# A third raw weight buffer from the second chunk on, low parts of weights in program order, and operands loaded whole

## The chip, the cores and the metric

The kernel runs on one core of a Trainium2 chip. The metric is the device time of one execution in microseconds (us). Three runs of the kernel before took 1780.84, 1779.01 and 1780.94 us; their median is 1780.84.

The engines are named as in the profile: PE is TensorE (matrix products), PEld its weight loads, DVE is VectorE, ACT is ScalarE, POOL is GpSimd, SP is SyncE. SP does no arithmetic here; it issues most of the transfers (DMAs), and its instructions, like those of each engine, run strictly one behind the other. A DMA that has to wait holds up what is behind it in its queue. SPq in the profile's rows is this queue.

## The reference

One layer of a streaming encoder is applied to a prompt of 1024 frames and to a sample of 32 frames that share the weights; the model dimension is 1024 and all numbers are 32 bit floats. Cut to its core:

```python
h = rms_norm(x, g_mix)
z = h @ w_in                       # q, k, v, conv h/B/C, gates a and b
a = attn_core(q, k, v) @ w_attn_out
bo = (cb * conv) @ w_conv_out      # short causal convolution over cc * ch
x = x + (sigmoid(ga) * a + sigmoid(gb) * bo) @ w_mix_out
hc = rms_norm(x, g_cross)          # cross-attention to 256 memory tokens,
cq = hc @ w_cq                     # 4 heads of 64
p = softmax(cq . mem_k * 0.125)
x = x + (p . mem_v) @ w_co
hm = rms_norm(x, g_mlp)
x = x + square(relu(hm @ w_up)) @ w_down   # 1024 -> 4096 -> 1024
```

A final norm follows, and the new keys, values and convolution rows are outputs too.

## The kernel before, in words

**Columns and chunks.** The 1056 frames (prompt and sample together) are the columns of the moving operand. They are worked on in three chunks of 384, 384 and 288 columns; `c` in the code is the chunk. The model dimension is on the 128 partitions, in eight tiles (`f` from 0 to 7).

**High and low parts.** To keep 32 bit precision each operand is split into a high part, which TensorE takes at its fast 32 bit rate, and the low rest. A product is three matmuls: weight high by operand high, weight high by operand low, weight low by operand high (lines 193 to 195 for whole chunks of the trunk, 864 to 866 in the first half of the MLP). `split` makes the parts: ScalarE copies the raw tile into the high part (`wh` for a weight, line 129), VectorE subtracts that from the raw one for the low part (`wl`, line 130).

**Weights.** A weight comes as a tile of 128x1024, 512 KB. `fetch_w` issues its load into a raw buffer (line 155), `issue_w` splits it; two weights are prepared ahead of the one in use (`LOOK`). Raw tiles `wr` rotate over two buffers; while the dictionary `third` is filled, each third fetch goes into a tile of another pool instead (tag `ws`, named wr with two numbers in the order listings). That pool, `W["pool"]`, is shared with work on sums of weights, which GpSimd does and stores to DRAM (`usum_d`, `gsum_d`, `wsum_d`), so a tile of it is free only when such a store has read it. For the odd weights of the trunk the low part is stored to DRAM once (`wl_d`, line 172) and loaded again by later chunks (line 166), with the high part cast at line 167.

**Phases.** First the input projection and the windowed attention (up to about 640 us), then pairs of gate products (to about 800). Then the trunk, chunk by chunk: eight products with w_conv_out, eight with w_mix, from 809 us on; beside the trunk of chunk 1 goes the cross-attention of chunk 0, beside the trunk of chunk 2 that of chunk 1. From about 960 us on, products of a first part of w_up fill in as well; from about 1072 us on only they do, beside the cross-attention of chunk 2. The second part of w_up begins at about 1196 us, w_down at 1436.

**Cross-attention.** `do_cq` makes the queries: ScalarE and VectorE split them (lines 1113 and 1114). For a unit, `scores` issues score matmuls `sc` into one PSUM bank, VectorE takes the negative maximum `nmx` (1143), ScalarE the exponentials `S` (1145, with a load of its function table where another function came before), VectorE the reciprocal `rec` (1146) and the multiplications (1148). `turn` transposes them on TensorE (`pt`, 1157) and splits them, and `values` makes the products `o`. Then come the products with w_co (1203).

**The first part of w_up.** It works on half of the columns, in two quarters of 264: `xa[0]` and `xa[1]`. The operands come from `normed(c, f)` (line 1279), which also stores the normed chunk to DRAM (`xn_d`, line 1282). The second quarter, `xa[1]`, is columns 264 to 527 and so has 120 columns of chunk 0 and 144 of chunk 1. Its raw values are gathered in the tile of its low part (in a `Z` tile): 120 columns from xn_d at `open_first` (line 1229), 144 straight from the tile of `normed(1, f)` (line 1284). `second_split(f)` then splits them in place (lines 1296 and 1297).

**What sets the order.** Python code calls the operations in a program order, which is a list of items (`plan`) with small calls placed at numbered fillers (`then(i, ...)`). A scheduler behind it then orders each engine's instructions by its own estimate of times, and may move an instruction ahead of others on its engine. `pin` forbids that for one instruction: it has to stand behind the instruction of its engine that the program issued just before it.

Of the kernel before, what the change touches and what calls it, by code (L numbers as in the profile page):

```python
# [10 lines left out]
F32 = mybir.dt.float32  # L11
# [11 lines left out]
CH = [(0, 384), (384, 384), (768, 288)]  # L23
NF = 8
HT = 528
QT = 264
# [14 lines left out]
def hybrid_step(ctx: ExitStack, tc: tile.TileContext, io):  # L41
    nc = tc.nc
    act, dve, pool_e, pe, sp = nc.scalar, nc.vector, nc.gpsimd, nc.tensor, nc.sync
# [38 lines left out]
    xn_d = dram.tile([P, NF, NT], F32, name="xn_d")  # L82
# [14 lines left out]
    def pin(ins):  # L97
        return tc.keep_in_program_order(ins)
# [19 lines left out]
    def item(fn, *keys):  # L118
        plan.append((fn, keys))
        worder.extend(keys)  # L120
# [4 lines left out]
    ready = []  # L125
    wpos = [0]

    def split(hi, lo, src):
        act.copy(hi, src)  # L129
        dve.tensor_sub(lo, src, hi.bitcast(F32))  # L130

    def weight(key):
        name, *at = key
# [11 lines left out]
    third = {}  # L145
# [12 lines left out]
    def issue_w():  # L158
        if not fetched:
            fetch_w()  # L160
        raw = fetched.pop(0)
        key = worder[wpos[0]]
        hi = wp.tile([P, 1024], F32R, tag="wh", name=nm("wh"))
        lo = wp.tile([P, 1024], F32R, tag="wl", name=nm("wl"))
        if kept.get(key) is not None:
            sp.dma_start(lo.bitcast(F32), kept[key])
            act.copy(hi, raw)
        else:
            split(hi, lo, raw)
            if key in kept:  # L170
                kept[key] = dram.tile([P, 1024], F32, name=nm("wl_d"))
                sp.dma_start(kept[key], lo.bitcast(F32))
        ready.append((worder[wpos[0]], (hi, lo)))
        wpos[0] += 1
# [101 lines left out]
    W = {}  # L276
# [514 lines left out]
    def pump(n):  # L791
        for into, at, t, get in coming:
            hi, lo = into[at] = (get(), get())
            pin(act.copy(hi, t))
            pin(dve.tensor_sub(lo, t, hi.bitcast(F32)))
        coming.clear()
        for into, at, src, cols, get in wanted[:n]:
            t = cols() if callable(cols) else tmp(cols)
            sp.dma_start(t, src)
            coming.append((into, at, t, get))  # L800
        del wanted[:n]
# [216 lines left out]
    def after_gates():  # L1018
        nonlocal m_cm, mpool, cr_cm, cr
        assert not pieces and "new" not in W  # L1020
        closed(x_cm)
        xacc_tile()
        third.update(n=0, pool=W["pool"])
        m_cm, mpool = opened("mpool", bufs=18, reuse_waits="tile")
        cr_cm, cr = opened("cross", bufs=1, reuse_waits="tile", side="right")

# [194 lines left out]
    def open_first():  # L1221

        closed(m_cm)
        S["l"] = ctx.enter_context(tc.tile_pool(name="first", bufs=4, reuse_waits="tile"))
        S["z"] = ctx.enter_context(tc.tile_pool(name="second", bufs=8, reuse_waits="tile"))
        for f in range(NF):
            z = zslot()
            xa[1][f] = (quarter(z, 0), quarter(z, 1))
            sp.dma_start(xa[1][f][1].bitcast(F32)[:, : CH[0][1] - QT], xn_d[:, f, QT : CH[0][1]])
        for name in ("w_cq", "w_co"):  # L1230
            del kept[name, 1]

# [44 lines left out]
    def normed(c, f):  # L1277
        t = tmp(CH[c][1])
        pin(dve.scalar_tensor_tensor(t, x1[c][f], col(G_MLP + f), R[c], op0=ALU.mult, op1=ALU.mult))
        o, n = CH[c]  # L1280
        if c < 2 or f > 3:
            sp.dma_start(xn_d[:, f, o : o + n], t)
        if c == 1:
            sp.dma_start(xa[1][f][1].bitcast(F32)[:, CH[0][1] - QT :], t[:, : HT - CH[1][0]])
        if c == 2:
            top[f] = t
        if c == 0:
            hi, lo = (yslot(0)[:, :QT] for _ in range(2))
            xa[0][f] = (hi, lo)
            act.copy(hi, t[:, :QT])  # L1290
            pin(dve.tensor_sub(lo, t[:, :QT], hi.bitcast(F32)))

    def split_here(hi, lo):

        raw = lo.bitcast(F32)
        pin(act.copy(hi, raw))
        pin(dve.tensor_sub(lo, raw, hi.bitcast(F32)))

    def second_split(f):
        split_here(*xa[1][f])  # L1300
# [329 lines left out]
    def beside(steps, fillers, late=()):  # L1630
        for i, filler in enumerate(fillers):
            item(*filler)
            for x in [x for at, x in late if at == i]:
                item(lambda x=x: x())
            if steps:
                kind, what = steps.pop(0)
                for x in what:
                    if kind == "items":
                        item(*x)
                    else:  # L1640
                        item(lambda x=x: x())
        return steps
# [10 lines left out]
    trunks[0].insert(NF, trunks[1].pop(0))  # L1653
    left = beside([], trunks[0], [(i, lambda: pump(2)) for i in range(NF)])
    item(lambda: pump(0))
    left = beside(cross_steps(0), trunks[1])

    normeds = lambda c, at: [(at + f, lambda f=f: normed(c, f)) for f in range(NF)]
# [12 lines left out]
    def then(i, *what):  # L1671
        at.setdefault(i, []).extend(what)
# [14 lines left out]
    assert opened_at == 18  # L1687
    then(18, call(open_first))
    for f in range(NF):
        then(19 + f // 4, call(normed, 1, f))  # L1690
        then(22, call(second_split, f))
    then(19, call(chunk_col, 2))
    then(20, call(chunk_row, 2))
# [291 lines left out]
```

## Time and profile before

| | us |
|---|---|
| median of three runs | 1780.84 |
| profiled execution | 1778.09 |
| its span, first to last instruction | 1776.3 |
| PE busy | 1734.2 (98%) |
| VectorE busy | 1184.4 (67%) |
| ScalarE busy | 852.8 (48%) |
| GpSimd busy | 576.8 (32%) |

The profiled execution is one of the program's own; its span leaves out 1.8 us before the first and after the last instruction. Matmuls are pipelined: one of 264 columns is listed with some 0.28 us, but the next starts 0.12 us after it. The granted clock is the share of its full speed that TensorE was given; its mean over the execution is 0.99. In the rows of the timeline the first number is the start in us from the start of the span, the second the duration; at the end, in brackets, how long the engine had stood idle, and behind the arrow whom it had waited for.

### The profile page before, as it was taken

Reading aid. Unit: us, or ns where it says so; the run is one execution under the profiler, and the core shown is the slowest. Engines: PE = TensorE matmul, PEld = TensorE weight load, DVE = VectorE, ACT = ScalarE, POOL = GpSimd, SP = SyncE. Lnnn points to the kernel's source line nnn. Section 1 sums busy time; section 2 is a strip of 40 time slices with the busy share of each in tenths; the row PEclk is TensorE's granted clock in tenths of the full one; section 3 lists DMA queues with packets and bytes.
Section 4 is the critical chain, followed back from the end, with each engine's and each line's share of the span. In section 5 each row is a group of like instructions: output and inputs, shape, how many; then the busy total and the mean of one; then the engine's idle time right before and its main releaser. Section 6 shows DMA issues by size and latency. Waiting matters only on the chain.

```text
span 1776.3 us, 32569 instructions
## 1 busy us (share of the span) xinstructions
PE 1734.2 (98%) x12250; PEld 1716.3 (97%) x12250; DVE 1184.4 (67%) x2270; ACT 852.8 (48%) x1660; POOL 576.8 (32%) x651
## 2 busy tenths in 40 slices
PE   8999999999999999979999999999999999999998
PEld 8999999999999999979999989999999999999998
DVE  7776867868666647536667677786666686556575
ACT  8643534435335324324556665774444463333443
POOL 0025366543453444531225130004555510000121
PEclk9999999999999999989999998999999999999999
DMA  5333334333446888747765667575666686554554
GB/s 183 109 117 128 111 128 155 120 139 136 148 155 223 298 274 288 264 166 272 261 213 196 236 224 233 183 257 196 223 221 224 213 310 212 186 184 167 193 173 157
DMA packets 182221, 349.75 MB, mean 197 GB/s; under 512 B 19744, under 2 KB 102976, under 8 KB 181936
## 3 DMA queue, kind: packets, MB, share of 16 engines
q1 hardware_dynamic: 167008, 295.07, 49.1%
q0 software_dynamic: 15056, 52.60, 8.4%
q8 instruction: 96, 1.57, 0.4%
q14 instruction: 61, 0.50, 0.1%
HBM read 252.82 MB, written 94.19 MB: 195 GB/s over the span
## 4 chain that ended last, share of the span: by engine, by line
PE 77%; DMA 11%; POOL 6%; DVE 2%; issue 2%; ACT 2%; SPq 0%; DVEq 0%; POOLq 0%; ACTq 0%
PE acc L193 10%; PE acc L195 10%; PE acc L194 10%; PE acc L1772 6%; PE acc L1770 6%; PE acc L1771 6%; PE acc L864 5%; PE acc L866 5%; PE acc L865 5%; DMA wsum_d<-ws 3%; DMA wsum_d<-xacc 3%; POOL ws L719 2%; POOL xacc L719 2%; PE pc L864 2%; PE pc L865 2%
## 5 line engine op out<-in xcount | busy, mean ns | idle before, releaser
L129 ACT CAST wh<-wr 128x1024 fp32r<-128x1024 f32 x226 | 237.2, 1050 | 424.5 <-PE acc L1771 126.2
L130 DVE TENSOR_TENSOR wl<-wr,wh 128x1024 fp32r<-128x1024 f32 x226 | 292.5, 1294 | 140.6 <-ACT wh L129 138.6
L193 PE MATMUL acc<-X,wh 128*128 128x384 f32 (+1 forms) x864 | 281.8, 326 | 6.6 <-ACT wh L129 6.6
L194 PE MATMUL acc<-X,wh 128*128 128x384 f32 (+1 forms) x864 | 279.1, 323 | 0.0
L195 PE MATMUL acc<-X,wl 128*128 128x384 f32 (+1 forms) x864 | 278.5, 322 | 0.3 <-DVE wl L130 0.3
L269 POOL TENSOR_TENSOR xacc<-xacc,ct 128x384 f32<-128x384 f32 (+1 forms) x56 | 73.4, 1314 | 401.8 <-ACT ct L267 400.3
L193 PEld LDWEIGHTS acc<-X,wh 128*128 128x128 f32 x864 | 163.0, 189 | 7.2 <-ACT wh L129 6.6
L194 PEld LDWEIGHTS acc<-X,wh 128*128 128x128 f32 x864 | 163.1, 189 | 0.7
L195 PEld LDWEIGHTS acc<-X,wl 128*128 128x128 f32 x864 | 162.8, 188 | 0.9 <-DVE wl L130 0.8
L195 PE MATMUL acc<-Y,wl 128*128 128x384 f32 (+1 forms) x432 | 139.1, 323 | 1.8 <-DMA wl<-wl_d 1.8
L193 PE MATMUL acc<-Y,wh 128*128 128x384 f32 (+1 forms) x432 | 138.8, 323 | 0.4 <-ACT Y L774 0.4
L194 PE MATMUL acc<-Y,wh 128*128 128x384 f32 (+1 forms) x432 | 139.1, 322 | 0.0
L1770 PE MATMUL acc<-n,wh 128*128 128x264 f32 x352 | 100.2, 285 | 0.0
L1771 PE MATMUL acc<-n,wh 128*128 128x264 f32 x352 | 100.1, 284 | 0.0
L1772 PE MATMUL acc<-n,wl 128*128 128x264 f32 x352 | 100.0, 285 | 0.1
L129 ACT CAST PTh<-pt 128x512 fp32r<-128x512 f32 (+3 forms) x94 | 46.0, 516 | 111.6 <-PE pt L582 110.8
L719 POOL TENSOR_TENSOR ws<-ws 128x256 f32<-128x256 f32 x100 | 91.9, 919 | 5.6
L719 POOL TENSOR_TENSOR xacc<-xacc 128x256 f32<-128x256 f32 x100 | 87.9, 879 | 5.5 <-DMA xacc<-in_w_in 0.2
L195 PEld LDWEIGHTS acc<-Y,wl 128*128 128x128 f32 x432 | 81.1, 188 | 2.1 <-DMA wl<-wl_d 2.1
L193 PEld LDWEIGHTS acc<-Y,wh 128*128 128x128 f32 x432 | 80.9, 188 | 0.7 <-ACT Y L774 0.7
L194 PEld LDWEIGHTS acc<-Y,wh 128*128 128x128 f32 x432 | 81.1, 188 | 0.0
L864 PE MATMUL acc<-n,wh 128*128 128x264 f32 x256 | 72.9, 285 | 0.8 <-DVE Z L1502 0.8
(422 smaller groups left out, 5511.5 us busy)
## 6 DMA issues: line engine op xcount, KB each, us to landing
wr<-in_w_in SPq DMA_DIRECT2D x53, 512.0 KB, 3.7
wr<-in_w_up SPq DMA_DIRECT2D x53, 512.0 KB, 4.5
wr<-wsum_d SPq DMA_DIRECT2D x40, 512.0 KB, 3.4
wr<-in_w_conv_out SPq DMA_DIRECT2D x24, 512.0 KB, 4.3
wr<-in_w_mix SPq DMA_DIRECT2D x24, 512.0 KB, 4.8
wr<-in_w_down SPq DMA_DIRECT2D x24, 512.0 KB, 3.4
wl<-wl_d SPq DMA_DIRECT2D x18, 512.0 KB, 4.6
n_d<-Z SPq DMA_DIRECT2D x32, 264.0 KB, 4.3
```

The source lines that it names most:

```text
L129: act.copy(hi, src)
L130: dve.tensor_sub(lo, src, hi.bitcast(F32))
L193: pe.matmul(out, wh[:, a], hi, start=(k == 0), stop=False)
L194: pe.matmul(out, wh[:, a], lo, start=False, stop=False)
L195: pe.matmul(out, wl[:, a], hi, start=False, stop=(k == len(acts) - 1))
L719: pin(pool_e.tensor_tensor(t[:, to], t[:, x], t[:, y], op=ALU.add))
L864: pe.matmul(acc, wh[:, a], hi, start=(start and k == 0), stop=False, skip_group_check=True)
L865: pe.matmul(acc, wh[:, a], lo, start=False, stop=False, skip_group_check=True)
L866: pe.matmul(acc, wl[:, a], hi, start=False, stop=(k == 3), skip_group_check=True)
L1770: pe.matmul(a, wh[:, s], hi, start=(t == 0 and k == 0), stop=False, skip_group_check=True)
L1771: pe.matmul(a, wh[:, s], lo, start=False, stop=False, skip_group_check=True)
L1772: pe.matmul(a, wl[:, s], hi, start=False, stop=(t == 1 and k == 7), skip_group_check=True)
```

## The change

There are three parts.

1. `third` is filled later. It was done in `after_gates`, ahead of the trunk of chunk 0; now it is an item of its own behind that trunk and a `pump(0)`. The trunk of chunk 0 has two raw buffers, and the count of fetches starts there.
2. `split` gets a flag `ordered`, set for weights while `third` is filled with `W["pool"]`, that is from the trunk of chunk 1 to `open_late`. With it the subtraction for the weight's low part is pinned: on VectorE it stands behind the last operation of the item that the program issued before it.
3. The low operand tile of `xa[1]` is no longer gathered by two DMAs of 120 and 144 columns. A new `second_load(f)` loads all 264 columns from xn_d, at filler 20, and all eight `normed(1, f)` stand at filler 19 (before, the first four at 19 and the last four at 20).

```diff
-    def split(hi, lo, src):
+    def split(hi, lo, src, ordered=False):
         act.copy(hi, src)
-        dve.tensor_sub(lo, src, hi.bitcast(F32))
+        sub = dve.tensor_sub(lo, src, hi.bitcast(F32))
+        if ordered:
+            pin(sub)
...
-            split(hi, lo, raw)
+            split(hi, lo, raw, "n" in third and third["pool"] is W["pool"])
...
         xacc_tile()
-        third.update(n=0, pool=W["pool"])
...
             xa[1][f] = (quarter(z, 0), quarter(z, 1))
-            sp.dma_start(xa[1][f][1].bitcast(F32)[:, : CH[0][1] - QT], xn_d[:, f, QT : CH[0][1]])
...
-        if c == 1:
-            sp.dma_start(xa[1][f][1].bitcast(F32)[:, CH[0][1] - QT :], t[:, : HT - CH[1][0]])
...
+    def second_load(f):
+        sp.dma_start(xa[1][f][1].bitcast(F32), xn_d[:, f, QT:HT])
...
     item(lambda: pump(0))
+    item(lambda: third.update(n=0, pool=W["pool"]))
     left = beside(cross_steps(0), trunks[1])
...
-        then(19 + f // 4, call(normed, 1, f))
+        then(19, call(normed, 1, f))
+    for f in range(NF):
+        then(20, call(second_load, f))
         then(22, call(second_split, f))
```

The arithmetic is the same, on the same engines. Line numbers of the kernel after are two higher than before from the function `split` to the end of `normed`. GpSimd's order stays as it was; that of the other engines is the same up to the trunk of chunk 0 and again from about 1200 us on. In SyncE's queue the load at 778.99 us of the profile into the first free `ws` tile (before, `wr_1614_9467<-in_w_conv_out`) is `wr_1809_10255<-in_w_cq` after, in the same row of the queue. The numbers behind a name only tell tiles apart; the same tile's number after is 8 lower, in the last two places below.

The first place is VectorE at the queries of chunk 1 (990 to 1000 us): `wl_11385` is the low part of a weight of the trunk of chunk 2, the `Y` rows of line 1114 (1115 after) the low parts of the queries. Before:

```order
L130 TENSOR_TENSOR wl_11385<-wr_11382,wh_11384 128x1024
L130 TENSOR_TENSOR M_11340<-ct_11336,M_11339 128x288
L1109 TENSOR_SCALAR ct_11374<-acc_11349,R_11290 128x384
L1109 TENSOR_SCALAR ct_11413<-acc_11388,R_11290 128x384
L1114 TENSOR_TENSOR Y_2068_11376<-ct_11374,Y_2068_11376 64x384
L1114 TENSOR_TENSOR Y_2069_11379<-ct_11374,Y_2069_11379 64x384
L1114 TENSOR_TENSOR Y_2075_11415<-ct_11413,Y_2075_11415 64x384
```

and after:

```order
L130 TENSOR_TENSOR M_11340<-ct_11336,M_11339 128x288
L1110 TENSOR_SCALAR ct_11374<-acc_11349,R_11290 128x384
L1110 TENSOR_SCALAR ct_11413<-acc_11388,R_11290 128x384
L1115 TENSOR_TENSOR Y_2068_11376<-ct_11374,Y_2068_11376 64x384
L1115 TENSOR_TENSOR Y_2069_11379<-ct_11374,Y_2069_11379 64x384
L130 TENSOR_TENSOR wl_11385<-wr_2070_11382,wh_11384 128x1024
L1115 TENSOR_TENSOR Y_2075_11415<-ct_11413,Y_2075_11415 64x384
```

The subtraction moved from ahead of the queries' scaling to behind two of their four splits.

The second place is SyncE's queue where the normed chunk 1 is stored and the operands of the second quarter are gathered (1078 to 1090 us). Before, a piece of the rows, in which each store has its copy into `Z` behind it:

```order
L1310 DMA s_d<-lt_12549 128x264
L155 DMA wr_2376_12685<-in_w_up 128x1024
L1282 DMA xn_d<-ct_12508 128x384
L1284 DMA Z_12453<-ct_12508 128x144
L1282 DMA xn_d<-ct_12512 128x384
L1284 DMA Z_12455<-ct_12512 128x144
```

and after, from the fifth store on:

```order
L1282 DMA xn_d<-ct_12512 128x384
L1282 DMA xn_d<-ct_12515 128x384
L1298 DMA Z_12453<-xn_d 128x264
L1282 DMA xn_d<-ct_12518 128x384
L1282 DMA xn_d<-ct_12521 128x384
L1298 DMA Z_12454<-xn_d 128x264
L1298 DMA Z_12455<-xn_d 128x264
L1298 DMA Z_12456<-xn_d 128x264
L1298 DMA Z_12457<-xn_d 128x264
L1298 DMA Z_12458<-xn_d 128x264
L1298 DMA Z_12459<-xn_d 128x264
L1298 DMA Z_12460<-xn_d 128x264
```

The loads stand in one row behind the stores that they read, and the load of the up weight that stood ahead of the first store (`wr_2376_12685`, after `wr_12677`) comes behind them, after one more store of `b_d`.

The third place is the first unit of the cross-attention of chunk 2 (1100 to 1124 us), on VectorE and on TensorE. On VectorE, `wl_12872` and `wl_12911` (after `wl_12864` and `wl_12903`) are low parts of up weights, `nmx`, `rec` and `S` the softmax of the unit. Before, from 1101.5 us on (the softmax's rows follow 15 rows further down):

```order
L130 TENSOR_TENSOR wl_12872<-wr_2414_12869,wh_12871 128x1024
L1328 TENSOR_SCALAR lt_12790<-lt_12790 128x264
L1327 TENSOR_TENSOR lt_12880<-acc_12878,lt_12879 128x264
L130 TENSOR_TENSOR wl_12911<-wr_12908,wh_12910 128x1024
L130 TENSOR_TENSOR mkl_12836<-mkr_12832,mkh_12835 128x256
L1328 TENSOR_SCALAR lt_12880<-lt_12880 128x264
```

and after:

```order
L130 TENSOR_TENSOR mkl_12835<-mkr_12831,mkh_12834 128x256
L1328 TENSOR_TENSOR lt_12911<-acc_12909,lt_12910 128x264
L1329 TENSOR_SCALAR lt_12911<-lt_12911 128x264
L1144 TENSOR_REDUCE nmx_12848<-sc_12838 128x4
L1147 RECIPROCAL rec_12850<-den_12849 128x4
L1149 TENSOR_SCALAR S_12847<-S_12847,rec_12850 128x256 x4
L130 TENSOR_TENSOR wl_12864<-wr_12861,wh_12863 128x1024
L130 TENSOR_TENSOR wl_12903<-wr_2421_12900,wh_12902 128x1024
```

Both subtractions now stand behind the whole softmax of the unit. On TensorE the last score matmul of the unit (`sc_12846`, after `sc_12838`) had behind it before, until the next unit's scores, 43 matmuls of up blocks (rows 6740 to 6782), and these end like this:

```order
L864 MATMUL acc_13290<-Y_2116_11584,wh_13125 128x264
L865 MATMUL acc_13290<-Y_2117_11585,wh_13125 128x264
L866 MATMUL acc_13290<-Y_2116_11584,wl_13126 128x264
L1140 MATMUL sc_12947<-mkh_10152,Y_2374_12679 128x256
L1140 MATMUL sc_12947<-mkl_10153,Y_2374_12679 128x256
```

After, the same stretch is:

```order
L1141 MATMUL sc_12838<-mkl_12835,Y_2389_12768 128x256
L866 MATMUL acc_13084<-Z_12453,wh_12902 128x264
L867 MATMUL acc_13084<-Z_12453,wh_12902 128x264
L1141 MATMUL sc_12939<-mkh_10152,Y_2374_12671 128x256
L1141 MATMUL sc_12939<-mkl_10153,Y_2374_12671 128x256
L1141 MATMUL sc_12939<-mkh_10152,Y_2374_12671 128x256
L1141 MATMUL sc_12939<-mkl_10153,Y_2374_12671 128x256
L1158 MATMUL pt_12954<-ident,S_12847 128x128
L1158 MATMUL pt_12963<-ident,S_12847 128x128
```

Two matmuls stand between the unit's last score and the next unit's, and the transposes `pt` of the first unit's softmax come directly behind; the up blocks follow them.

## The prediction

> **What bounds the kernel now.** I read the page's busy times first, then the busy time of PE in stretches, then the list of what PE waited for, then the timelines at the places that the order moves. From the page:
>
> ```profile
> PE 1734.2 (98%) x12250; PEld 1716.3 (97%) x12250; DVE 1184.4 (67%) x2270; ACT 852.8 (48%) x1660; POOL 576.8 (32%) x651
> ```
>
> TensorE is busy for 98% of the span, and the change neither adds nor removes a matmul. So the question is only how long PE stands, or runs at a lower clock, in the stretch that the change touches. The order of all engines is the same up to the trunk of chunk 0 and from about 1200 us on; between them lie 850 to 1200 us of the profile. The table of stretches (start and end; elapsed; busy time and count of PE, PEld, DVE, ACT, POOL; granted clock; DMA share; GB/s):
>
> ```profile
> 776.00:790.00 14.00, 4.62 (x15) 4.19 (x15) 4.32 (x7) 4.57 (x7) 0.49 (x1) 0.58 0.83 285
> 850.00:895.00 45.00, 42.26 (x242) 41.16 (x241) 26.16 (x40) 21.70 (x37) 9.51 (x9) 1.00 0.74 259
> 895.00:990.00 95.00, 95.00 (x587) 94.86 (x586) 64.57 (x116) 56.01 (x107) 34.44 (x28) 1.00 0.60 210
> 990.00:1047.00 57.00, 52.82 (x376) 50.31 (x375) 47.56 (x93) 39.29 (x85) 12.02 (x13) 1.00 0.60 204
> 1080.00:1104.00 24.00, 21.04 (x143) 20.43 (x142) 18.55 (x40) 12.68 (x28) 0.00 (x0) 0.86 0.78 263
> 1096.60:1100.00 3.40, 3.40 (x16) 3.40 (x17) 2.95 (x4) 3.20 (x6) 0.00 (x0) 0.50 0.79 302
> 1100.00:1104.00 4.00, 4.00 (x25) 4.00 (x25) 2.97 (x6) 1.04 (x3) 0.00 (x0) 0.68 0.45 140
> 1104.00:1124.00 20.00, 20.00 (x166) 19.89 (x166) 15.14 (x26) 11.86 (x23) 0.00 (x0) 1.00 0.74 245
> 1124.00:1150.00 26.00, 24.52 (x197) 23.62 (x196) 17.05 (x45) 19.85 (x60) 0.00 (x0) 1.00 0.43 140
> ```
>
> From 850 us (895 to 990 has no loss at all) PE stands 2.74 + 4.18 + 2.96 + 0 + 1.48 = 11.4 us. That is most of what a better order can win by gaps, and the list of PE's waits from 850 to 1225 us (total, times, longest) says who ends them:
>
> ```profile
> PE acc L864 <- ACT lt L1324: 2.3, 1, 2.3
> PE acc L193 <- DVE Ga L1065: 1.9, 1, 1.9
> PE acc L195 <- DMA wl<-wl_d: 1.8, 1, 1.8
> PE acc L864 <- ACT lt L1354: 1.5, 1, 1.5
> PE acc L195 <- DVE wl L130: 1.2, 3, 0.5
> ```
>
> Only 1.2 us are waits for the low part of a weight, which is what the new order on VectorE governs; the others are single waits for an eviction or a load.
>
> **The third buffer, and the large stall that it does not touch.** The 9.38 us that PE stands in 776 to 790 us come from SyncE's queue:
>
> ```profile
> 752.34 0.33 SPq L155 DMA_DIRECT2D wr<-in_w_in  x1
> 778.99 0.33 SPq L155 DMA_DIRECT2D wr<-in_w_conv_out  x1
> ```
>
> The queue stands from 752.67 to 778.99 at the load of a conv_out weight into a ws buffer that is not free. In the new order that row is still there, at the same place and into a ws buffer, only now it carries a w_cq weight. So I cost this at nothing. What the later start does cost is in the trunk of chunk 0, which has two raw buffers for each weight instead of three, so that each load starts one load later. The nearest row:
>
> ```profile
> 874.57 1.11 SPq L1076 DMA_DIRECT2D mkr<-in_cmem_k  x2
> ```
>
> The load of the kept low part, for which PE waits 1.8 us, now stands behind one more such pair of key loads: 1.1 us later, and nothing is ahead of PE to hide it, so **+1.1**. Bounds: 0, if the queue reaches it earlier because one weight load fewer stands ahead, to 2.2, if the other waits for a wl of that stretch double as well.
>
> **The pinned low parts, first place: the queries of chunk 1.** VectorE's rows:
>
> ```profile
> 991.75 1.22 DVE L130 TENSOR_TENSOR wl<-wr,wh 128x1024 fp32r<-128x1024 f32 x1 [0.28 <-ACT wh L129]
> ...
> 996.59 2.31 DVE L1114 TENSOR_TENSOR Y<-ct,Y 64x384 fp32r<-64x384 f32 x4
> ```
>
> ```profile
> 996.44 0.30 PE L195 MATMUL acc<-Y,wl 128*128 128x288 f32 x1
> ```
>
> The subtraction that ran in VectorE's idle time at 991.75 now stands behind two of the four Y splits, which start at 996.59 and end 1.16 later, so it starts at 997.75 and its result is there at 998.97. PE used it first at 996.44. The new PE order has work of 0.27 (two matmuls of the next weight) and 0.88 (six score matmuls) to put in between, but the scores wait for the first two splits too: they start at 997.2 and end at 998. So PE stands about 0.6 before the scores and 1.0 behind them, 1.6, of which I take **+1.4** because later waits in that stretch (the 1.9 for Ga) swallow some. Bounds: 0 to 3, double that, since the next unit repeats the pattern.
>
> **The operands loaded whole.** Rows of SyncE's queue and of PE, and from the page the mean of a cast and the median from issue to landing:
>
> ```profile
> 1078.00 0.38 SPq L155 DMA_DIRECT2D wr<-in_w_up  x1
> 1078.47 0.44 SPq L1282 DMA_DIRECT2D xn_d<-ct  x1
> ...
> 1088.73 0.47 SPq L1284 DMA_DIRECT2D Z<-ct  x1
> ```
>
> ```profile
> 1091.92 0.36 PE L864 MATMUL acc<-Z,wh 128*128 128x264 f32 x1 [0.32 <-ACT R L252]
> ```
>
> ```profile
> L129 ACT CAST wh<-wr 128x1024 fp32r<-128x1024 f32 x226 | 237.2, 1050 | 424.5 <-PE acc L1771 126.2
> ...
> wr<-in_w_up SPq DMA_DIRECT2D x53, 512.0 KB, 4.5
> ```
>
> Eight small loads and the eight Z<-ct copies leave the queue; eight loads of 128x264 come in, each behind the landing of its own store of xn_d. The w_up load that goes out at 1078.00 now stands behind all of them. Worked out: the 16 issues from 1078.47 to the end of the last, 1089.20, are 0.67 apart; six stores go out until 1082.5, the first load waits for the first store's landing, at 4.5 like a weight's until 1083.0, the last two stores follow until 1085.0, the last load waits until about 1089, and the weight goes out near 1090. It lands 4.5 later and is cast 1.05 later, at 1095.5. PE wanted it at 1091.9: a wait of 3.6. The waits of before in that place, 0.32 (the row above), 0.36 and 2.3 for lt, are 3.0, for evictions that stood behind other work of ACT. PE itself comes 2.5 later by the two terms above. One takes the place of the other: **0**. Bounds: -5.4, if the weight is not late and the low clock behind that wait goes too (priced below), to +3, if the old waits stay beside the new one. The eight DMA issues saved, 0.5 each, are worth nothing: while the queue waits for landings, nobody gets them back.
>
> **The pinned low parts, second place: the scores of chunk 2.** This carries the forecast. Rows of PE, VectorE and ACT, in that order:
>
> ```profile
> 1115.35 0.28 PE L1140 MATMUL sc<-mkl,Y 128*128 128x256 f32 x1
> 1120.79 0.39 PE L1140 MATMUL sc<-mkh,Y 128*128 128x256 f32 x1
> ```
>
> ```profile
> 1115.66 1.23 DVE L1143 TENSOR_REDUCE nmx<-sc 128x4 f32<-128x1024 f32 x1
> ...
> 1120.77 0.18 DVE L1146 RECIPROCAL rec<-den 128x4 f32<-128x4 f32 x1 [1.94 <-ACT S L1145]
> 1120.99 1.14 DVE L1148 TENSOR_SCALAR S<-S,rec 128x256 f32<-128x256 f32 x4
> ```
>
> ```profile
> 1117.51 1.28 ACT L1145 ACT_TABLE_LOAD   x1
> 1118.81 0.47 ACT L1145 ACTIVATE S<-sc,nmx 128x256 f32<-128x256 f32 x1
> ```
>
> Before, the low part of the up weights was ready long ahead, and PE did up blocks from the last score matmul (ends 1115.63) to the next scores (1120.79): no time was lost in 1104 to 1124. Now the subtractions for the next two up weights stand behind the whole softmax, so PE's order can put only two matmuls, 0.24, behind the last score, then the next four scores, which wait for the exponentials because they write the same bank, and then the transposes, which wait for the four multiplications. Chain from the last score: reduction until +1.26, the four exponentials until the reciprocal starts, 1118.81 to 1120.77, so until +3.2; PE stands 2.95. The next scores take 0.5 of that time (four of 0.12 each); the multiplications end at 1122.13, 1.36 after the reciprocal starts, and PE comes some 0.3 behind them: 1.2 more. Together 4.1, if the table load is done before the reduction ends, and 5.4 if not. I take 4.1, since ACT has nothing ahead of it then.
>
> Behind such a wait comes a second price, in the two stretches of the table behind the 2.3 us wait for lt, which ended at 1096.5 (granted clock 0.50, then 0.68). At clock 1.00 PE did 166 matmuls in 20 us, 8.3 each us; here it did 16 instead of 28 and 25 instead of 33, which is 1.5 + 1.0 = 2.4 us lost at the lower clock. The 1.9 us wait for Ga had none of this (990 to 1047 has clock 1.00). My two waits are 2.95 and 1.2, the first longer than the one that lowered it: **+6.5** in all. Bounds: 1.2, if only the second wait is left, to 8.
>
> The Trainium skill ("TensorE: Matmul & The Clock Gate", section "HAM oscillation — how this bites in real kernels") says that the clock falls to half after PE idles for longer than about 3.4 us. By that rule neither of my two waits would lower it, and the forecast would be 2.4 lower, 1785.9. The row behind the 2.3 us wait disagrees with it, so the sum keeps the 2.4; the rule's case lies inside the forecast's own range, and about a third of the forecast's chance is on that side.
>
> **The rest, to 1200 us.** Rows of SyncE's queue (first and last of 16 loads for the sums):
>
> ```profile
> 1147.88 0.32 SPq L1241 DMA_DIRECT2D t<-xn_d  x1
> ...
> 1155.96 1.18 SPq L1244 DMA_DIRECT2D n<-xn_d  x1
> ```
>
> The co matmuls are now in whole blocks behind two other blocks, so the 1.48 us that PE stood in the stretch from 1124 should go: **-1.5**. Against it, these 16 loads, 9.3 us of queue, now stand ahead of an up weight that used to go first; I cost it at nothing, since no raw weight's load, nor a cast behind one, stands in the list of what PE waited for; if that cover is gone it is up to +5, half of the 9.3.
>
> **Sum:** 1.1 + 1.4 + 0 + 6.5 - 1.5 = +7.5 us. The profiled execution took 1778.09 (span 1776.3 and 1.8 around it), so 1785.6 in its terms. It lies 2.75 below the median of the three runs, 1780.84; on the median it is 1788.3, 0.42% more. About 0.2% (3.6 us) is what a measurement of this kernel can tell from no change.
>
> **Rivals.**
> - *The pins pay.* Before, VectorE takes up a low part early and so stands waiting for its cast, and evictions that PE needs queue behind it. In program order those evictions come first: the waits for lt, Ga and wl in the list go (2.3 + 1.9 + 1.2 = 5.4), the 2.4 at the lower clock with them, and the 1.5 from 1124. If the scores of chunk 2 stay covered, the sum is 1.1 - 9.3 = -8.2: 1772.6. For it: these waits are real. Against it: at the scores VectorE has the low parts behind the softmax and PE has 0.24 us of other work. It decides if the exponentials end less than about 1 us after the last score. 0.16.
> - *The waits at 1091 to 1096 go and the rest comes:* the third part at -5.4, sum +2.1, 1782.9. For it: eight copies and their issue leave. Against it: the weight near 1090. Within 0.2%: 0.18.
> - *SyncE's queue is the bound:* the w_up load late beside the old waits (+3) and the weight behind the 16 loads (+5): +15.5, 1796.3. For it: each of the eight loads waits for a landing. Against it: before, the queue stood 26 us at one load and PE only 9.4 of it. 0.16.
> - That the change does not do what it says has a part in the first: the stall at 776 stays, so no gain of 9.4 comes from the later buffer.
>
> **How the numbers follow.** The forecast (+3.6 to +12) has 0.50; slower is 0.50 + 0.16 = 0.66, same 0.18, faster 0.16. The likeliest alone: 1784.5 to 1793. The range reaches down nearly to the gain's case and up past the queue's, 1776 to 1801, and leaves out most of the 0.16 and some 0.04 above.
>
> **What would show it.** In the profile after: a wait of about 3 us of PE at sc for ACT S near 1110 to 1115, then about 1 us at pt for DVE S, and a granted clock well under 1 right behind; the 9.4 us at 776 as before; wl<-wl_d nearer 3 than 1.8; the w_up load behind the eight Z loads near 1090; no wait for Y at the co matmuls. Wrong: if the stretch 1104 to 1124 keeps PE full, or if 776 to 790 changes.

## The result and the profile after

The kernel after is slower: 1792.4 us median of 14 runs (1782.43 to 1797.62) against 1778.65 for the kernel before in as many runs beside it; ratio 1.0073, 95% interval 1.0059 to 1.0087. That is some 13 us more, where 7.5 were forecast. The profiled execution took 1782.43 us, the lowest of the 14, so its profile shows less than the median has; the last experiment asks why.

The busy times on the page of the kernel after, and the table of stretches (as shown of before, with 1047 to 1080 added, and with 1116.1 to 1120, right behind the wait at the scores, in place of the two short ones):

```profile
PE 1737.7 (98%) x12250; PEld 1717.1 (96%) x12250; DVE 1176.7 (66%) x2270; ACT 855.5 (48%) x1660; POOL 571.7 (32%) x651
```

```profile
776.00:790.00 14.00, 12.46 (x67) 12.23 (x68) 7.45 (x11) 7.08 (x11) 0.00 (x0) 0.88 0.64 223
850.00:895.00 45.00, 41.90 (x238) 40.33 (x237) 25.79 (x41) 24.40 (x39) 10.58 (x10) 1.00 0.65 220
895.00:990.00 95.00, 93.17 (x575) 92.71 (x574) 62.44 (x111) 55.19 (x104) 29.83 (x28) 1.00 0.59 207
990.00:1047.00 57.00, 52.28 (x345) 48.40 (x344) 45.42 (x89) 36.16 (x79) 10.25 (x11) 0.91 0.59 195
1047.00:1080.00 33.00, 31.02 (x212) 30.06 (x211) 18.00 (x33) 17.99 (x29) 12.14 (x11) 0.95 0.59 213
1080.00:1104.00 24.00, 20.16 (x142) 19.30 (x141) 18.78 (x42) 12.38 (x27) 0.00 (x0) 0.93 0.75 249
1104.00:1124.00 20.00, 16.23 (x115) 15.19 (x115) 12.94 (x27) 10.60 (x25) 0.00 (x0) 0.91 0.56 176
1116.10:1120.00 3.90, 3.88 (x18) 3.45 (x19) 3.86 (x8) 0.48 (x2) 0.00 (x0) 0.59 0.11 19
1124.00:1150.00 26.00, 26.00 (x218) 26.00 (x218) 17.98 (x43) 17.92 (x51) 0.00 (x0) 1.00 0.57 190
```

PE stood 9.4 us in the first of these stretches before and 1.5 now; it was full from 1104 to 1124 and now stands 3.8, at a clock of 0.59 behind; it stood 1.5 from 1124 and is now full. What PE waited for from 850 us on in the kernel after:

```profile
PE sc L1141 <- ACT S L1146: 3.2, 1, 3.2
PE acc L197 <- DVE wl L130: 2.5, 5, 0.7
PE acc L1204 <- DVE Ga L1208: 1.8, 1, 1.8
PE o L1177 <- DVE tO L1180: 1.8, 2, 1.4
PE acc L197 <- DMA wl<-wl_d: 1.6, 1, 1.6
PE acc L866 <- ACT lt L1355: 1.5, 1, 1.5
PE pq L226 <- POOL xacc L271: 1.4, 1, 1.4
```

The first row is the wait that the prediction rests on. To see where time goes in many kernels with the same matmuls, the starts of the n-th matmul can be compared. The table is worked out from the traces: how much later (+) than in the profile of before the n-th matmul starts, in us. The first two columns are n and its start before. Where the orders differ, the n-th matmul is not the same one, which blurs a row by some tenths; in before and after, rows 4900 to 5540 and 7800 are the same matmuls with the same ones ahead of them.

```
   n   before    after  e1 pins  e2 third  e3 loads  e4 no    e5 early  e10 late  e9 not      e7 before,  e6 after,
                        alone    alone     alone     pins     pins      pins      at scores   ws in order ws in order
4900   766.89   - 0.66  + 1.62   + 2.15    - 0.13    + 1.72   + 2.73    + 3.10    + 0.79      + 0.90      + 1.86
5100   811.52   - 9.22  + 0.98   + 2.43    - 1.14    + 2.44   + 1.76    + 2.42    + 0.21      -11.62      -10.67
5540   891.73   - 6.23  + 2.50   + 4.54    + 1.60    + 2.41   + 3.68    + 4.11    + 2.74      - 9.76      - 6.69
5920   954.59   - 5.82  + 2.70   + 5.30    + 1.60    + 2.90   + 4.56    + 4.38    + 2.70      - 6.94      - 6.13
6000   968.47   - 3.67  + 6.35   + 5.30    + 1.60    + 2.90   + 6.70    + 4.38    + 4.74      - 6.94      - 0.20
6280  1009.04   - 2.96  + 7.06   + 4.61    + 0.88    + 3.02   + 7.42    + 3.63    + 4.57      - 7.69      + 0.50
6620  1062.82   + 3.19  +13.35   + 4.99    - 0.02    + 5.84   +14.35    + 4.99    + 7.84      - 6.27      + 5.06
6900  1105.64   + 3.29  +21.50   + 5.31    + 1.46    + 6.00   +12.12    + 5.77    + 7.94      - 6.38      + 4.95
6960  1112.92   + 9.68  +27.19   + 5.31    + 1.48    + 6.02   +12.14    +12.49    +11.67      - 6.34      +10.01
7300  1159.17   + 4.91  +22.78   + 4.65    + 2.26    + 7.44   +14.01    + 8.06    + 7.04      - 6.56      + 5.26
7600  1198.80   + 4.94  +22.52   + 3.51    + 2.18    + 7.40   +12.49    + 6.71    + 7.77      - 7.84      + 5.30
7800  1226.56   + 4.95  +19.45   + 3.53    - 0.88    + 4.35   + 9.45    + 3.66    + 4.73      -10.90      + 5.34
```

In the column of the kernel after, 8.6 us are won between 4900 and 5100 and 14.2 lost from there on (from -9.22 to +4.95). The median's 13 is close to the 14.2; that the 8.6 is not in it is inferred below.

### The profile page after: what moved, and what is told of

Same layout as the page of the kernel before. It is cut to its first block, busy times and chain, and to the rows that moved or that the text cites. A ratio compares the mean times of both kernels' runs of the same rounds, so it can differ in the third digit from the quotient of the medians.

```text
span 1780.7 us, 32529 instructions
## 1 busy us (share of the span) xinstructions
PE 1737.7 (98%) x12250; PEld 1717.1 (96%) x12250; DVE 1176.7 (66%) x2270; ACT 855.5 (48%) x1660; POOL 571.7 (32%) x651
## 4 chain that ended last, share of the span: by engine, by line
PE 76%; DMA 10%; POOL 6%; DVE 3%; issue 2%; ACT 2%; SPq 0%; DVEq 0%; ACTq 0%; POOLq 0%
PE acc L197 10%; PE acc L195 10%; PE acc L196 10%; PE acc L1774 6%; PE acc L1776 6%; PE acc L1775 6%; PE acc L868 4%; PE acc L866 4%; PE acc L867 4%; DMA wsum_d<-ws 3%; POOL ws L721 2%; DMA wsum_d<-xacc 2%; POOL xacc L721 2%; PE pc L866 2%; PE pc L868 2%
```

## The experiments

**The parts alone.** Three kernels do one part each. The first pins low parts from the trunk of chunk 1 on (a flag is set by an item there), with the third buffer and the loads as before:

```diff
-            split(hi, lo, raw)
+            split(hi, lo, raw, bool(inorder) and "n" in third and third["pool"] is W["pool"])
...
     item(lambda: pump(0))
+    item(lambda: inorder.append(1))
```

> Only the low parts of weights are kept in program order on VectorE, from the trunk of chunk 1 on; the third buffer starts as before and the operands are gathered as before. Theory (the pins make the loss, place by place): the waits of PE that the profile after has and the one before has not, at the scores of chunk 2 (3.2 us), at the queries and values of chunk 1 (about 4.4 us from 1015 to 1035), at the co products of chunk 0 (1.8) and at the sums behind 1060 (1.4), are there; the kernel is 9 to 12 us slower than before. Rival 1 (the later third buffer makes the loss, since all loads come later): within 3 us of before. Rival 2 (the pins help and the other two parts hurt): 3 to 8 us faster.

Measured: 1796.02 us, ratio 1.0099 (1.0082 to 1.0117), 18 us. The pins make the loss, and more than the whole change does. The excess stands in one place: from row 6620 to 6900, 8.2 us against 0.1 in the kernel after, where PE waits 5.9 us for the high part of an up weight. (3 us of it come back near 1200 us, by another order of TensorE that is described below.)

The second moves only the `third.update` (the first two lines of this diff), the third makes only the whole loads with all `normed(1, f)` at filler 19 (the others, with the two removed DMAs as in the change):

```diff
-        third.update(n=0, pool=W["pool"])
+    item(lambda: third.update(n=0, pool=W["pool"]))
...
-        then(19 + f // 4, call(normed, 1, f))
+        then(19, call(normed, 1, f))
+        then(20, call(second_load, f))
```

> Only the start of the third raw buffer is moved behind the trunk of chunk 0. Theory: trunk of chunk 0 costs 2 to 4 us more (waits for the low parts and the merged gates from 835 to 885), nothing behind it: +2 to +4 us in all. Rival 1: 10 us or more slower. Rival 2: the load at the ws buffer no longer holds SyncE's queue at 752 to 779 us, and the kernel is up to 9 us faster.

> Only the low operand tile of the second quarter is loaded whole, with all eight normed at one filler. Theory: waits at 1085 to 1105 change their names but not their sum; within 3 us of before. Rival: the w_up load behind the eight loads comes late and costs 3 to 6 us with a lower clock behind it.

Measured: 1779.34 us, ratio 1.0016 (0.9997 to 1.0034), and 1779.6 us, ratio 1.0010 (0.9989 to 1.0030). Both intervals include no change. The trunk of chunk 0 (rows 5100 to 5540) costs 2.1 more with the later buffer, but 2.7 more with the whole loads alone, where the buffer starts as before. In the profiles of all kernels here but one, PE has the same order in these rows, and against before they lose from 0.0 (no pins) to 4.0 (the kernel after with the ws load in order). So single profiles cannot tell a cost of the later buffer there from this scatter.

**The two parts without the pins:** the kernel after, with

```diff
-            split(hi, lo, raw, "n" in third and third["pool"] is W["pool"])
+            split(hi, lo, raw)
```

> The changed kernel without the pins: the third buffer starts later and the operands are loaded whole. Theory (the pins alone make the loss; the parts alone gave 1.0016 and 1.0010): 0 to 4 us above before, and no wait at sc for ACT S near 1113 us. Rival (the parts only hurt together, since the whole loads stand behind stores in a queue that has one raw buffer less to look ahead): 6 us or more above before.

Measured: 1782.07 us, ratio 1.0006 (0.9995 to 1.0018). From here to 1.0073 it is 12 us, the pins' price; 3 of the 12 turn out below to be another order of TensorE near 1200 us.

**Pins for a part of the time.** The first kernel clears the flag at filler 20, so that the pins end ahead of the queries and scores of chunk 2; the second sets it only there.

```diff
-            split(hi, lo, raw, "n" in third and third["pool"] is W["pool"])
+            split(hi, lo, raw, bool(inorder) and "n" in third and third["pool"] is W["pool"])
...
+    then(20, call(inorder.clear))
     then(21, lambda: item(do_cq(2, 0), ("w_cq", 0)))
```

```diff
+    then(20, call(inorder.append, 1))
     then(21, lambda: item(do_cq(2, 0), ("w_cq", 0)))
```

> The changed kernel with the pins ended at filler 20, ahead of the queries and scores of chunk 2; up to there it is the changed kernel. Theory (the wait of 3.2 us at the scores of chunk 2 and the low clock behind it, 6.4 us by the trace, come from these pins; the co products behind gave 4.8 back, which they then don't): 2 to 6 us below the changed kernel, and that wait is gone from the profile. Rival 1 (all of the 6.4 is given back at the co products, since the work is only moved): as the changed kernel within 1.5 us. Rival 2 (the earlier pins make all of the loss): as the changed kernel, and the wait is still there or another has its place.

> The changed kernel with the pins only from filler 20 on, the other half of the run with the pins ended there (that was 6 us below the changed kernel and 5 to 6 above the two parts without pins). Theory (the places add up): 5 to 7 us above the two parts without pins (1.0006 of before), so a ratio to before of 1.0035 to 1.0045, with the wait of 3 us at sc for ACT S near 1113 to 1125, and PE without the waits of the changed kernel at 958 (Ga) and 1020 to 1032 (tO, Y, wl). Rival (the late pins only hurt since the early ones brought VectorE behind): ratio below 1.002 and no such wait.

Measured: early pins 1787.05 us, ratio 1.0040 (1.0025 to 1.0055); late pins 1778.83, ratio 1.0000 (0.9986 to 1.0015). The first fits the theory's number, the second does not fit its own: the wait at the scores is there with the late pins and costs nothing in the end. The profile of the kernel with late pins, the list of PE's waits and then the stretches at that place:

```profile
PE sc L1142 <- ACT S L1147: 2.8, 1, 2.8
```

```profile
1114.90:1117.80 2.90, 0.08 (x2) 0.04 (x1) 0.06 (x1) 2.80 (x9) 0.00 (x0) 0.86 0.14 49
1117.80:1122.00 4.20, 4.06 (x17) 3.66 (x18) 4.16 (x9) 0.48 (x3) 0.00 (x0) 0.50 0.16 35
```

In the table, against the kernel without pins: +6.7 from row 6900 to 6960 and -5.9 from 6960 to 7300. Up to 7300 PE has caught up, because waits that the kernel without pins has from 1124 us on, most of them at the co products, are gone:

```profile
PE acc L1204 <- DVE Gb L1208: 1.6, 1, 1.6
PE acc L1204 <- ACT Y L1186: 1.1, 1, 1.1
PE acc L1204 <- ACT lt L1355: 0.8, 1, 0.8
```

The work that could not be done ahead of the scores is done ahead of co. The wait was moved, and only its difference stays.

Late pins alone are worth nothing and early ones 6 us, but both together 12. Half of the missing 6 is in the last rows: from 7600 to 7800 before, after, the later buffer alone and the kernel after with the ws load in order (below) keep their distance to 0.04 us, and all the others win 3.05. There the second part of w_up begins, and in all of the others 24 matmuls of `acc<-t` stand in a row ahead of those of `pc<-n` on PE, where before and after have them mixed. It goes with no one part of the change: the planner (the scheduler that orders the engines) comes to one of two orders there, and the kernels before and after have the slower one. So 3 us of each comparison between a kernel of the one kind and one of the other are this order: the pins at their places cost about 9 of the 12 us, and some 21 where they are alone. The last 3 us of the missing 6 lie within the intervals.

**Not pinned right behind scores.** A weight that is issued as the next thing after `scores` of a unit is left free; all others stay pinned.

```diff
+    scored = []
...
-            split(hi, lo, raw, "n" in third and third["pool"] is W["pool"])
+            split(hi, lo, raw, not scored and "n" in third and third["pool"] is W["pool"])
...
-            fn(*[next_w(k) for k in keys])
+            ws = [next_w(k) for k in keys]
+            scored.clear()
+            fn(*ws)
...
             self.stl = stl
+            scored.append(1)
```

> The changed kernel, but a weight that is issued right behind the scores of a cross-attention unit is not pinned; all others are. In the order the low parts of the two up weights stand ahead of the softmax of chunk 2's first unit again, and those beside chunk 1's units ahead of their softmax. Theory (a pinned low part hurts where the operation that it is pinned to is the end of a softmax, which PE waits for too): the wait at sc near 1113 is gone, and part of the loss from 1015 to 1035; 5 to 9 us below the changed kernel. Rival 1 (what hurts is that low parts are pinned at all near the cross-attention, behind whatever): the next low part in the row takes that place, with a wait for wl or S of 2 us or more near 1110 to 1125; less than 3 us below the changed kernel.

Measured: 1782.67 us, ratio 1.0025 (1.0013 to 1.0037), 9.7 below the kernel after. Of that 3.05 is the planner's order at the second part again; the rest, 6.6, is at chunk 1's units (rows 6280 to 6620: +3.3 instead of +6.2), at chunk 2's first unit (+3.7 instead of +6.4) and in the trunk. The wait at sc is still there in another form, 1.95 us for a key's high part (ACT mkh). The theory holds by size for most of the pins' loss; that the wait there goes was wrong, and the rival had foretold another in its place (for wl or S).

**The load that holds the queue at 752.** Four kernels keep the first load into a ws buffer in program order on SyncE's queue. It then stands in the trunk of chunk 0 (or later, with the later buffer) and not ahead of the last loads of the gate products:

```diff
-        sp.dma_start(raw.rearrange("p (i c) -> p i c", i=4) if len(src.shape) == 3 else raw, src)
+        load = sp.dma_start(raw.rearrange("p (i c) -> p i c", i=4) if len(src.shape) == 3 else raw, src)
+        if third and third["n"] == 3 and third["pool"] is W.get("pool"):
+            pin(load)
```

> The kernel before, with the first load into a ws buffer kept in program order on SyncE's queue, so that it stands in the trunk of chunk 0 and not ahead of the last loads of the gate products. Theory: PE's wait of 9.4 us at 776 in the profile before, which was 1.5 in the profile after with the same order there, depends on how far GpSimd is when the queue reaches that load; without the load there it is gone, the low clock behind it too: 5 to 12 us faster than before, and the runs lie closer together than 10 us. Rival: the next load that stands in that place waits for a raw buffer just as long; same as before.

> The changed kernel with the first load into a ws buffer in program order on SyncE's queue. Theory (the wait at 776 is in nearly all executions of both kernels, and the profile after shows one of the few where GpSimd was early; what the change costs lies behind it): about 9 us below the changed kernel, some 1783, so still 13 to 15 us above the kernel before with the same edit (1768.7), and the profile has no wait near 776. Rival (the wait at 776 covers part of the loss behind it, because loads get ahead while PE stands): less than 5 us below the changed kernel.

> The changed kernel without the pins and with the first load into a ws buffer in program order: the two other parts and that edit. Theory: as the kernel before with that edit alone, 1766 to 1772. Rival: with the third buffer started late that load is far from need and nothing collides behind it, so a few us better, 1760 to 1765.

> The changed kernel with the pins only from filler 20 on and the first load into a ws buffer in program order. Theory (late pins alone cost nothing, ratio 1.0000, and the edit is worth 0.5 to 0.6%): 1766 to 1772, as the two kernels with that edit and no pins. Rival (the late pins are only harmless while PE stands at 776): 1773 or more.

Measured, as ratios to before: before with that edit 0.9946 (0.9926 to 0.9967), 1768.74 us; after with it 1.0012 (1.0001 to 1.0023), 1780.95 us; no pins 0.9947 (0.9930 to 0.9964), 1769.71 us; late pins 0.9936 (0.9922 to 0.9950), 1767.72 us. Three of them beat both kernels by about 10 us and cannot be told from each other. Against the kernel after, no pins and late pins, each without the edit, the edit wins 11.4, 12.4 and 11.1 us, and there nothing but SyncE's queue from 770 to 893 us is in another order. In the kernel before it wins 9.5, but there the planner ordered PE, VectorE and ScalarE anew from 820 to 1240 us as well, and 3 us of the 9.5 are the order near 1200; so this pair alone does not show what the load costs. The stretch in the kernel before with the edit, where PE now never stands:

```profile
764.00:790.00 26.00, 26.00 (x165) 26.00 (x164) 13.38 (x19) 8.59 (x14) 12.15 (x14) 1.00 0.56 182
```

Between the pinned and the unpinned kernel with the edit (1780.95 and 1769.71) lie 11 us, as without it. So the two losses add: the queue's stall is in both kernels' medians, and the change's price is behind it.

**The changed kernel once more,** for a second profile:

> The changed kernel once more, unaltered, for a second profile of it. Theory (the wait at 776 depends on how far GpSimd is, and the first profile of this kernel caught one of its fastest executions): this profile shows the wait again, 8 to 11 us near 777, GpSimd's stores of the sums ending later than 770, and a profiled time of 1790 us or more; behind 800 us the waits are those of the first profile, name by name. Rival (the changed kernel has no such wait, and its median is high for what lies behind): no wait over 3 us near 777 again.

Measured: 1793.15 us median of 4, ratio 1.0086 (1.0067 to 1.0105). The expectation on the profile was wrong: its profiled execution, again the fastest of its runs with 1785.63, waits only 1.35 + 0.38 us near 778. Behind 800 us the longest waits are those of the first profile, 3.15 at sc among them; a few under 1.3 us are others. What is different at 776 is how far GpSimd is. Its last stores of the sums, which free the ws buffer, in before and in after:

```profile
775.05 1.45 POOL L723 DMA_DIRECT2D usum_d<-ws  x2 [0.41 <-POOL ws L719]
```

```profile
766.44 1.45 POOL L725 DMA_DIRECT2D usum_d<-ws  x2 [0.41 <-POOL ws L721]
```

and SyncE's queue in the profile after, which goes on 8.7 us earlier than before:

```profile
751.68 0.33 SPq L157 DMA_DIRECT2D wr<-in_w_in  x1
770.31 0.33 SPq L157 DMA_DIRECT2D wr<-in_w_cq  x1
```

The profiles of e1, e2, e3, e4, e5, e9 and e10 all have 9.1 to 10.3 us of wait there, and in every profile but the two of the kernel after these stores end between 776.0 and 781.1 us. That the unprofiled executions of the kernel after have it too is inferred, not seen: the edit that takes the load away brings its median down by 11.4 us, close to where its two profiled executions were, and no other wait of that size is there to take away. Why both profiled executions of this one kernel had an early GpSimd stays open.

## Why the prediction was right or wrong

- **The sign and the likeliest case** were right: slower, with a wait at the scores of chunk 2. The size was 13 instead of 7.5, a little above the +12 up to which the forecast's chance of 0.50 went. Part of this is luck: the places that the sum had priced come to 2.4 us by the table (0.7 + 0.1 + 6.4 - 4.8, without the trunk of chunk 0, which the scatter hides), less than the 3.6 that can be told from no change. Most of the loss is at places that were not priced.
- **The scores of chunk 2, +6.5:** right in mechanism and about in size; rows 6900 to 6960 give +6.4. That includes a wait of 0.6 for a key's high part, which the step did not have; the second profile of the kernel gives +4.9 there and the kernel after with the ws load in order +5.1, both without it. So 6.4 comes as close to 6.5 as it does by luck. The kernel after at that place, PE and then VectorE:

```profile
1112.29 0.28 PE L1141 MATMUL sc<-mkl,Y 128*128 128x256 f32 x1
1116.12 0.39 PE L1141 MATMUL sc<-mkh,Y 128*128 128x256 f32 x1 [3.16 <-ACT S L1146]
...
1116.82 1.94 PE L1158 MATMUL pt<-ident,S 128*128 128x128 f32 x8
```

```profile
1112.79 1.22 DVE L1144 TENSOR_REDUCE nmx<-sc 128x4 f32<-128x1024 f32 x1
1116.10 0.18 DVE L1147 RECIPROCAL rec<-den 128x4 f32<-128x4 f32 x1 [2.09 <-ACT S L1146]
1116.32 1.14 DVE L1149 TENSOR_SCALAR S<-S,rec 128x256 f32<-128x256 f32 x4
1117.38 2.35 DVE L130 TENSOR_TENSOR wl<-wr,wh 128x1024 fp32r<-128x1024 f32 x2
```

  The forecast wait was 2.95 and it is 3.16; the table load of ACT was hidden, as taken. The second wait of 1.2 is spread over the transposes, which took 1.94. Both low parts come after. The clock behind was 0.59 on the mean of 3.9 us; the step had priced it at 2.4 us from a like row.
- **The rest, -1.5:** the sign was right and the size too small. Rows 6960 to 7300 give -4.8: not only the wait for Y at the co products went, but also what followed it in the kernel before, a clock of 0.57 from 1150 to 1154 us and a wait of 0.4 for xacc. No wait for an up weight stands behind the 16 loads, as taken. So the place that carries the forecast is worth 6.4 - 4.8 = 1.6 in the end and not 5.0; late pins alone, with +6.7 - 5.9 in the table and a ratio of 1.0000, agree with that.
- **The operands loaded whole, 0:** right in sum (rows 6620 to 6900, +0.1), but not by the waits that were forecast. The steps can be seen in SyncE's queue, the up weight behind the loads at 1091.6 where about 1090 was worked out:

```profile
1086.52 3.27 SPq L1298 DMA_DIRECT2D Z<-xn_d  x7
1089.84 1.66 SPq L1311 DMA_DIRECT2D b_d<-lt  x1
1091.59 0.38 SPq L157 DMA_DIRECT2D wr<-in_w_up  x1
```

  The wait of 3.6 us for that weight did not come. PE's waits of 0.3 to 2.3 there, 3.0 in all, gave way to 1.2, 1.0, 1.0 and 0.8 us for lt, ct, Y and a low part, 3.8 in all (in the second profile, one of 1.2 is for a high part).
- **The queries of chunk 1, +1.4:** rows 5920 to 6280 give 2.9, of which 2.2 stand at 958 us, a place that the prediction does not have; the queries themselves cost some 0.7.
- **The third buffer, +1.1:** the wait for wl_d was to grow to 2.9 and is 1.6. Rows 5100 to 5540 lose 3.0, but a kernel without that part loses 2.7 and one with it 0.0, so a cost of the buffer of about 1 us is neither shown nor refuted.
- **What was left out,** and makes most of the difference: the co products of chunk 0 at 958 us (+2.2) and chunk 1's values and normed operands from 1009 to 1063 us (+6.2, with the 1.4 for xacc). At 958 the low part of a weight stands ahead of the additions into Ga in both kernels. Before, it ran ahead of the split of Y and took 1.23 us; the first addition started 2.3 us after the first co matmul (960.49):

```profile
961.60 1.23 DVE L130 TENSOR_TENSOR wl<-wr,wh 128x1024 fp32r<-128x1024 f32 x1
962.74 0.55 DVE L1207 TENSOR_TENSOR Ga<-acc,Ga 128x384 f32<-128x384 f32 x1
```

  After, it is pinned behind that split and takes 2.03 us; the first addition starts 4.5 us after the first co matmul (954.70), and PE waits 1.8 for it:

```profile
956.70 0.64 DVE L275 SCALAR_TENSOR_TENSOR Y<-Gb,prm,Y 128x384 fp32r<-128x384 f32 x1 [0.69 <-ACT Y L274]
957.25 2.03 DVE L130 TENSOR_TENSOR wl<-wr,wh 128x1024 fp32r<-128x1024 f32 x1
959.21 1.47 DVE L1208 TENSOR_TENSOR Ga<-acc,Ga 128x384 f32<-128x384 f32 x3
```

  From 1009 to 1063 there are smaller waits (0.4 to 1.4) for tO, Y, Ga, a low part and xacc, and a low clock, 0.50 in both of these stretches:

```profile
1028.00:1032.00 4.00, 2.05 (x6) 1.27 (x5) 3.38 (x7) 1.43 (x3) 1.61 (x2) 0.50 0.76 248
1032.00:1036.00 4.00, 3.89 (x16) 3.89 (x17) 2.54 (x6) 1.44 (x3) 0.71 (x1) 0.50 0.75 248
```

  Early pins alone bring the ratio from 1.0006 to 1.0040, 6 us, with these waits and without the one at the scores of chunk 2, so these places are shown to be the pins'. The step that failed is that pins were priced at two places out of about five; which instruction each of the small waits hangs on was worked out at 958 alone.
- **The stall at 776 "as before":** not in the profile after, which by the prediction's own words would speak against it; by the medians, as inferred above, it is as before in most executions.
- **The rivals.** "The pins pay" is refuted: alone they cost 18 us. Its waits for Ga and lt did go in part and others came. "SyncE's queue is the bound" does not show: rows 6620 to 6900 lose 0.1. "The waits at 1091 to 1096 go" is half true: 2.3 for lt became 1.2, and others came beside it.
- **The clock rule.** The Trainium skill ("TensorE: Matmul & The Clock Gate", section "HAM oscillation — how this bites in real kernels") has the clock fall to half after idle times of more than about 3.4 us. The traces do not bear that bound out: the clock was at 0.50 during or right behind waits of 2.3 (before), 3.16 (here), 2.8 (late pins) and 2.8 us (third later alone), and none of them reached 3.4. That the sum kept the 2.4 us was right in direction; but the clock did not fall after every wait as long as the 2.3 it was read from (2.5 us, at the end of this text), so that it fell here did not follow from that one row.

## What to carry to other kernels

An instruction that is pinned stands behind whatever the program happened to issue last on that engine; ask at every such place what that is, and above all whether it is the end of a chain (a softmax) that the consumer of the pinned result waits for too. A wait that is only moved is paid as a difference: before adding it to a sum, read what stands idle in the next 50 us, for that idle time pays it back. And a queue that runs strictly in order should not be given a load whose buffer is freed by another engine's slow work; holding one such load back won 11 to 12 us in the three pairs of kernels that differ in nothing else, and none of the three parts won anything. Where a planner makes the order, also compare the order in stretches that the edit does not touch: here another order near 1200 us is 3 us of several comparisons.

## What the runs showed of the hardware that had not been expected

In the clock records of all these traces the granted clock is either 1.00 or 0.50, and the stretches at 0.50 between 700 us and the last 10 us of the span last 3.4 us or a multiple of it (6.8, 10.2, 13.7). Values between, as 0.59 and 0.68, are means of stretches that hold both.

The length of a wait alone does not say whether the clock falls. It was 0.50 during or right behind each wait of 2.8 us or more between 850 and 1200 us, but a single wait of 1.8 us (no pins) had 0.50 behind it as well:

```profile
1022.72 0.61 PE L195 MATMUL acc<-M,wh 128*128 128x288 f32 x1 [1.77 <-ACT M L129]
```

```profile
1022.70:1026.10 3.40, 3.38 (x14) 3.38 (x15) 3.40 (x9) 3.17 (x11) 0.00 (x0) 0.50 0.35 113
```

One of 2.5 us (the whole loads alone) left it at 1.00:

```profile
886.29 0.44 PE L197 MATMUL acc<-Y,wl 128*128 128x384 f32 x1 [2.52 <-DMA wl<-wl_d]
```

```profile
886.30:890.00 3.70, 3.70 (x21) 3.70 (x22) 1.17 (x2) 1.97 (x3) 1.02 (x1) 1.00 0.92 365
```

After waits of 0.5 to 1.4 us close together (1025.9 to 1030.1 us in the kernel after) it was 0.50 for 10 us, from 1028.0 on. And the kernel before has 0.50 from 1065.0 to 1068.4 us with no wait over 0.3 us in the 7 us ahead of it; what ran there were sums over one column (`pq<-ones`) in a row. Why the clock fell there is not shown.

GpSimd's work on the sums, with the same instructions in the same order, ended at 767.9 us in one profile and at 776.5 in another (the ends of its last stores above). Between the two profiles TensorE won 8.6 us from the 4900th to the 5100th matmul. So an engine that is busy for a third of the time can move the whole kernel by some 9 us from one execution to another, where a queue waits for it.
